# Values of three attention branches computed with the sequence on partitions, in a layer kernel on one core

## Chip, cores, metric

The kernel runs on one core of a Trainium2 chip. A core has TensorE (PE: matrix products of a stationary operand, loaded by PEld, and a moving one, into banks of PSUM), VectorE (DVE), ScalarE (ACT), GpSimd (POOL) and SyncE (SP), whose queue here issues nearly all DMAs. Each engine carries out its own instructions in order and waits at semaphores for the others. The metric is device time in microseconds.

## What is computed

One layer of a hybrid encoder, sequence S = 1024, width D = 1024, all in float32:

```python
h = rmsnorm(x, g[0])
proj = h @ w_in[l]
(mq, mk, mv, mo, mi, mf, dq, dk, dv, rq, rk, rv, rg, gates) = split_in(proj)
qk = jax.nn.silu(causal_dwconv(concatenate([mq, mk]), mlstm_conv[l]))
hm = sigmoid(mo) * head_rms(mlstm(mq_c, mk_c, mv, mi + bias, mf + bias))   # 4 heads x 256
hd = rmsnorm(diff_attention(dq, dk, dv, lam)) * (1 - lam_init)             # 8 heads, values 128
hr = silu(rg) * head_rms(retention(rq, rk, rv))                            # 4 heads x 256
y = (gm * (hm @ w_mlstm_out) + gd * (hd @ w_diff_out) + gr * (hr @ w_ret_out)) @ w_out
x = x + rmsnorm(y, g[1])
a, u = split(rmsnorm(x, g[2]) @ w_ffn_in[l])
x = x + rmsnorm((silu(a) * u) @ w_ffn_out[l], g[3])
```

mlstm and retention are scans over chunks; diff_attention is softmax attention in blocks of 128 queries.

## The kernel before

**Products.** Each float32 operand is split into a high part and the rest (`split_sbuf`, lines 104 to 106: a cast on ACT, a subtraction on DVE, tiles wh and wl), and each product is three matmuls (`mm3`, lines 108 to 113). Large products go by the seven-product scheme of Strassen and Winograd. h transposed lies on chip, hT, as seven combinations (A11, A12, S1 to S4, A22) in both parts. A `Unit` makes 256 columns of proj (heads' q, k, o or v, the gates): each of seven products takes 12 matmuls of 128x512 with weight blocks stationary and hT moving, so results have channels on partitions. Weights come in tiles ws (line 317 subtracts one from another for the scheme). Evacuations add halves, and for the mLSTM's q and k run the convolution (lines 476 and 478) on DVE.

**Order of the stages.** x is normalised and turned (lines 262 to 281), and `begin` runs the first three units, v, o and q of head 0, while the second half of x is still being turned. `gate_products` and `gate_rows` (scans on DVE for the mLSTM's gates) follow, three dense steps to each of gate_rows' steps. Then `weave(core, rate)` takes steps of twelve matmuls from `dense` (all further units, later the merges) between the steps of a core: `mlstm_core`, `ret_core` (32 chunks of 128 positions each, 2.6 dense steps to each unit of weight, two units of weight to a chunk), `diff_core`. The products after the cores (`run_last`, the FFN, `down`) fill the rest.

**Values.** v of a unit is stored with channels on partitions, beside q, k and o, in m_dram or r_dram; `chunk_of` (line 643) loads one chunk of all four, ch, one chunk ahead. `natural_v` (line 663) turns v's two 128x128 blocks on PE through `natural` (line 653), and splits the result. For the differential branch `diff_values` (lines 510 to 521) turns four blocks in each of 16 evacuations.

**What sets the order.** The Tile framework's scheduler orders every engine's instructions from the data they need and the pools they rotate through: 32 big slots, 4 for ws, 5 for weight parts, 14 half tiles s2k, and PSUM as 4 banks for the cores and 4 ("d", `psum(True)`) for dense work. `issue_after` holds work behind an instruction. In `diff_core`, `turn` (line 860) transposes the softmax weights in two groups of up to four, copied by line 870. `down` (line 1190) makes operand parts in `make` (line 1239) and runs the last operands' matmuls in line with the norm at the end.

## Time and profile before

| | us |
|---|---|
| median of 3 runs | 2622.48 (2620.74 to 2623.88) |
| the profiled execution | 2623.93 |
| its span in the trace | 2622.1 |
| TensorE busy in it | 2518.1 (96%) |
| VectorE busy | 1648.1 (63%) |
| ScalarE busy | 1250.1 (48%) |
| GpSimd busy | 335.1 (13%) |

The span is what the trace covers; the 1.8 us beside it lie outside. A busy PE is not at its peak: matmuls overlap, and their ends are modelled. So a group's mean length is no price; the distance between starts is. Stretches of the span have different limits, and each is read by itself.

### The profile page before, as it was taken

To read this page: it belongs to the slowest core of one execution; us is meant where nothing else is said; L and a number is where in the kernel's file an instruction comes from. 1 tells how busy PE (TensorE), PEld (TensorE's weight loads), DVE (VectorE), ACT (ScalarE), POOL (GpSimd) and SP (SyncE) were. 2 spreads that over 40 slices of the span, in tenths; PEclk is the share of its full clock that TensorE was granted. 3 is DMA by queue.
4 is the path that set the end of the run, shared out by engine and by line. 5 is a ranking of instruction groups with operands and counts; after the bars stand their busy time and mean duration, and the time that the engine had idled before them with its cause. 6 is when DMAs were issued, how large, how long until landed. Compare 5 with 4: busy or idle time off the path is not lost.

```text
span 2622.1 us, 35166 instructions
## 1 busy us (share of the span) xinstructions
PE 2518.1 (96%) x12061; PEld 2056.0 (78%) x12061; DVE 1648.1 (63%) x3156; ACT 1250.1 (48%) x2564; POOL 335.1 (13%) x657
## 2 busy tenths in 40 slices
PE   6999999999999999999999988999999999999997
PEld 4777887888888888888878776778877888887885
DVE  6778778666656665656556566554368655656756
ACT  6564554544444444545455555552365333334444
POOL 0011111000000000000003223332121111111000
PEclk9999999999999999999999999999999999999999
DMA  4344444444455545444476666646443333327442
GB/s 127 91 129 125 123 137 142 129 129 143 135 143 162 153 149 155 134 132 129 129 214 157 157 182 163 176 157 202 145 137 112 102 99 102 101 97 276 125 134 92
DMA packets 402077, 368.92 MB, mean 141 GB/s; under 512 B 18957, under 2 KB 302046, under 8 KB 401898
## 3 DMA queue, kind: packets, MB, share of 16 engines
q1 hardware_dynamic: 399280, 364.19, 46.3%
q10 hardware_dynamic: 2618, 2.49, 0.3%
q8 instruction: 95, 1.56, 0.3%
q14 instruction: 84, 0.69, 0.1%
HBM read 249.92 MB, written 116.69 MB: 140 GB/s over the span
## 4 chain that ended last, share of the span: by engine, by line
PE 70%; issue 10%; DVE 5%; ACT 4%; POOL 3%; DMA 3%; SPq 0%; DVEq 0%; POOLq 0%; ACTq 0%
PE ps L112 21%; PE ps L113 21%; PE ps L111 21%; PE ps L841 1%; PE ps L878 1%; ACT sb L848 1%; POOL dfac L221 1%; PE ps L694 1%; DMA s2k<-branch 1%; PE ps L653 1%; DVE wl L106 1%; DVE sb L843 1%; POOL fv L220 1%; POOL xr L208 0%; PE ps L701 0%
## 5 line engine op out<-in xcount | busy, mean ns | idle before, releaser
L105 ACT CAST wh<-ws 128x512 fp32r<-128x512 f32 (+1 forms) x622 | 385.4, 623 | 729.0 <-PE ps L112 524.8
L106 DVE TENSOR_TENSOR wl<-ws,wh 128x512 fp32r<-128x512 f32 (+1 forms) x622 | 449.9, 726 | 271.5 <-ACT wh L105 256.2
L317 DVE TENSOR_TENSOR ws<-ws,ws 128x512 f32<-128x512 f32 x234 | 161.0, 690 | 111.1 <-DMA ws<-in_w_in_dram 63.8
L111 PE MATMUL ps<-bh,wh 128*128 128x512 f32 x384 | 155.3, 404 | 0.0
L112 PE MATMUL ps<-bl,wh 128*128 128x512 f32 x384 | 152.6, 397 | 0.2 <-DVE bl L106 0.2
L113 PE MATMUL ps<-bh,wl 128*128 128x512 f32 x384 | 152.3, 397 | 0.0
L330 ACT COPY s2k<-ps 128x512 f32<-128x512 f32 x234 | 135.4, 581 | 8.7 <-PE ps L113 8.4
L111 PE MATMUL ps<-A11h,wh 128*128 128x512 f32 x312 | 127.0, 407 | 1.6 <-ACT wh L105 1.5
L113 PE MATMUL ps<-A11h,wl 128*128 128x512 f32 x312 | 125.5, 402 | 2.7 <-DVE wl L106 2.7
L111 PE MATMUL ps<-S2h,wh 128*128 128x512 f32 x312 | 125.1, 403 | 2.7 <-ACT s2k L330 2.7
L111 PE MATMUL ps<-A12h,wh 128*128 128x512 f32 x312 | 125.0, 401 | 2.2 <-DVE s2k L458 2.2
L112 PE MATMUL ps<-wl,wh 128*128 128x512 f32 x308 | 120.6, 392 | 6.1 <-DVE wl L106 6.1
L112 PE MATMUL ps<-S1l,wh 128*128 128x512 f32 x312 | 123.6, 396 | 1.6 <-DVE S1l L106 1.6
L111 PE MATMUL ps<-S3h,wh 128*128 128x512 f32 x312 | 125.1, 401 | 0.0
L112 PE MATMUL ps<-A11l,wh 128*128 128x512 f32 x312 | 124.7, 400 | 0.1
L111 PE MATMUL ps<-A22h,wh 128*128 128x512 f32 x312 | 124.8, 400 | 0.0
L112 PE MATMUL ps<-A12l,wh 128*128 128x512 f32 x312 | 123.8, 397 | 0.9 <-DVE xv L207 0.5
L111 PE MATMUL ps<-S4h,wh 128*128 128x512 f32 x312 | 124.6, 399 | 0.0
L111 PE MATMUL ps<-S1h,wh 128*128 128x512 f32 x312 | 124.1, 401 | 0.4 <-ACT S1h L105 0.3
L112 PE MATMUL ps<-S2l,wh 128*128 128x512 f32 x312 | 124.4, 399 | 0.0
L113 PE MATMUL ps<-S2h,wl 128*128 128x512 f32 x312 | 123.7, 397 | 0.0
L112 PE MATMUL ps<-A22l,wh 128*128 128x512 f32 x312 | 123.6, 396 | 0.0
(303 smaller groups left out, 6428.8 us busy)
## 6 DMA issues: line engine op xcount, KB each, us to landing
ws<-in_w_in_dram SPq DMA_DIRECT2D x112, 512.0 KB, 4.5
ws<-in_w_ffn_in_dram SPq DMA_DIRECT2D x44, 512.0 KB, 4.0
m_dram<-s2k SPq DMA_DIRECT2D x64, 256.0 KB, 2.3
ch<-m_dram SPq DMA_DIRECT2D x32, 512.0 KB, 4.4
r_dram<-s2k SPq DMA_DIRECT2D x64, 256.0 KB, 2.3
ch<-r_dram SPq DMA_DIRECT2D x32, 512.0 KB, 4.8
qk_dram<-s2k SPq DMA_DIRECT2D x64, 256.0 KB, 2.2
dk<-qk_dram SPq DMA_DIRECT2D x64, 256.0 KB, 5.9
```

The lines of the kernel that those rows point to most:

```text
L105: nc.scalar.copy(hi, src)
L106: nc.vector.tensor_sub(lo, src, hi.bitcast(F32))
L111: nc.tensor.matmul(ps, lh, rh, start=start, stop=False, skip_group_check=more)
L112: nc.tensor.matmul(ps, lh, rl, start=False, stop=False, skip_group_check=more)
L113: nc.tensor.matmul(ps, ll, rh, start=False, stop=stop, skip_group_check=more)
L220: nc.gpsimd.tensor_scalar(t, ss, scale, extra, op0=ALU.mult, op1=ALU.add)
L221: nc.gpsimd.tensor_tensor(dst, t, expo[:, 0:1], op=ALU.pow)
L317: nc.vector.tensor_sub(*sub[r])
L330: nc.scalar.copy(t, ps)
L653: nc.tensor.transpose(ps[:, j * P:(j + 1) * P], ch[:, i + j, :], ident)
L694: nc.tensor.matmul(ps[:, :P], ch[:, 2 + j, :], ch[:, j, :], start=j == 0, stop=j == 1)
L841: nc.tensor.matmul(ps[:, :b - a], d["q", qb // 4][:, c, half_cols(qb)], d["k", n][i][:, c, :b - a], start=i == 0, stop=i == 1)
```

## The change

**Values.** `natural_columns` makes the 1024 value columns of one branch with the seven products, with column slices of hT stationary and the split weights moving (128x512), so that results have the sequence on partitions. It runs for mLSTM, differential and retention values, one after another and alone, between `gate_products` and `gate_rows`, with all eight PSUM banks, and stores to mv_dram, dv_dram and rv_dram. Twelve value units of 84 matmuls go; 3 x 336 come. `natural_v` and `diff_values` lose their transposes. A chunk is loaded by two DMAs. The first three units are now o, q and k of head 0, so two of them are convolved, and the weave's rate is 2.0.

**Loads.** The first weights are loaded in the order in which `begin` uses them, behind the second half of x; the early splits of unit 0 and unit 1 no longer stand ahead of `begin`.

**Others.** The second group of `turn` uses a "d" bank; `run_last` skips a step of `turns` at i = 0; the last four operand pairs of `down` go to big slots (oh), so all are held at the end.

```diff
-    m_dram = dram.tile([MH, P, 8, S], F32, name="m_dram")
-    r_dram = dram.tile([MH, P, 8, S], F32, name="r_dram")
+    m_dram = dram.tile([MH, P, 6, S], F32, name="m_dram")
+    r_dram = dram.tile([MH, P, 6, S], F32, name="r_dram")
+    mv_dram = dram.tile([S, D], F32, name="mv_dram")
+    rv_dram = dram.tile([S, D], F32, name="rv_dram")
...
+    def natural_columns(seven, w, dst):
+        raw = [pool.tile([P, D], F32, tag="ws", bufs=N_WS, name=nm("ws")) if k < 4 else big([P, D], name="ws") for k in range(KT)]
+        for k in range(KT):
+            nc.sync.dma_start(raw[k], w[k * P:(k + 1) * P, :])
+        def right(role, k):
+            (b11, b12), (b21, b22) = ((t[:, halfs(0)], t[:, halfs(1)]) for t in (raw[k], raw[k + 4]))
+            sub = {"T1": (b12, b12, b11), "T2": (b12, b22, b12), "T3": (b11, b12, b11), "T4": (b12, b21, b12)}
+            if role in sub:
+                nc.vector.tensor_sub(*sub[role])
+                return sub[role][0]
+            return {"B11": b11, "B21": b21, "B22": b22}[role]
+        order = [(l, r, k) for l, r in (("A11", "B11"), ("A12", "B21"), ("S1", "T1"), ("S2", "T2"), ("S3", "T3"),
+                                        ("S4", "B22"), ("A22", "T4")) for k in range(4)]
+        ready = []
+        def make(n):
+            while len(ready) < min(n, len(order)):
+                _, role, k = order[len(ready)]
+                ready.append(parts_tile([P, HALF]))
+                split_sbuf(*ready[-1], right(role, k))
+        step = [0]
+        def product(ps, more):
+            for _ in range(4):
+                n = step[0]
+                make(n + 4)
+                left, _, k = order[n]
+                for j in range(4):
+                    mm3(ps[j], cols_at(seven.slot(left, k), j * P, (j + 1) * P), ready[n], k == 0 and not more, k == 3, more)
+                ready[n] = None
+                step[0] += 1
+                yield
+        def kept(ps):
+            t = [half_tile() for _ in range(4)]
+            for j in range(4):
+                nc.scalar.copy(t[j], ps[j])
+            return t
+        def out(sh, ch, ps, part):
+            for j in range(4):
+                if part is None:
+                    t = half_tile()
+                    nc.scalar.copy(t, ps[j])
+                else:
+                    t = part[j]
+                    nc.vector.tensor_add(t, ps[j], t)
+                nc.sync.dma_start(dst[(sh * 4 + j) * P:(sh * 4 + j + 1) * P, halfs(ch)], t)
+        x = [psum(True) for _ in range(4)]
+        yield from product(x, False)
+        a = kept(x)
+        y = [psum() for _ in range(4)]
+        yield from product(y, False)
+        out(0, 0, y, a)
+        y = [psum() for _ in range(4)]
+        yield from product(y, False)
+        e = kept(y)
+        yield from product(x, True)
+        b = kept(x)
+        yield from product(x, True)
+        out(1, 1, x, e)
+        yield from product(y, True)
+        out(0, 1, y, b)
+        yield from product(x, True)
+        out(1, 0, x, None)
...
-    def diff_values(hp):
-
-        def evac(j, sh, ps, part):
-            t = total(ps, part)
-            tr = psum()
-            for i in range(4):
-                nc.tensor.transpose(tr[:, i * P:(i + 1) * P], t[:, i * P:(i + 1) * P], ident)
-            v = half_tile()
-            nc.scalar.copy(v, tr)
-            c = (hp * 2 + j) * P
-            nc.sync.dma_start(dv_dram[halfs(sh), c:c + P].rearrange("(i p) e -> p i e", p=P), v.rearrange("p (i e) -> p i e", i=4))
...
-        c = u["c"]
-        nc.sync.dma_start(t, src[u["hd"]][:, :, c * P:(c + 1) * P])
+        c, hd = u["c"], u["hd"]
+        nc.sync.dma_start(t[:, 0:6, :], src[0][hd][:, :, c * P:(c + 1) * P])
+        nc.sync.dma_start(t[:, 6:8, :].rearrange("p j e -> p (j e)"), src[1][c * P:(c + 1) * P, hd * HD:(hd + 1) * HD])
...
-        ps = natural(ch, 6)
-        split_sbuf(t[:, 0, :HD], t[:, 1, :HD], ps)
+        split_sbuf(t[:, 0, :HD], t[:, 1, :HD], ch[:, 6:8, :].rearrange("p j e -> p (j e)"))
...
-        need(first + 4)
+        need(first + 3)
...
-                ps = psum()
+                ps = psum(g == 1)
...
-                        next(turns[0], None)
+                        if i > 0:
+                            next(turns[0], None)
...
-                o = [parts_tile([P, HALF]) for _ in range(2)]
+                if k < len(order) - 4:
+                    o = [parts_tile([P, HALF]) for _ in range(2)]
+                else:
+                    hl = [big([P, 2, HALF], F32R, "oh") for _ in range(2)]
+                    o = [tuple(x[:, i, :] for x in hl) for i in range(2)]
...
-        q, k, o, v = head(m_dram, (C_MQ, C_MK, C_MO, C_MV),
+        q, k, o = head(m_dram, (C_MQ, C_MK, C_MO),
                           (lambda dst, hd: convolved(dst, 2 * hd), lambda dst, hd: convolved(dst, 8 + 2 * hd),
-                           lambda dst, hd: stored(dst, AF.Sigmoid), lambda dst, hd: stored(dst)), hd)
-        units += [v, o, q, k]
+                           lambda dst, hd: stored(dst, AF.Sigmoid)), hd)
+        units += [o, q, k]
...
-        units.append(of((C_DV + hp * HD, C_DV + hp * HD + P), diff_values(hp)))
...
     units[0].load(0)
-    units[0].load(1)
     load_x(4)
-    for u in units[1:3]:
-        u.load(0)
-        u.load(1)
+    for u, i in ((1, 0), (2, 0), (0, 1), (1, 1), (2, 1)):
+        units[u].load(i)
...
-    with tc.issue_after(marks[-1].ins):
-        with tc.issue_after(lows[-1].ins):
-            units[0].split("T1")
-            units[1].split("B11", "B21")
-    begin(units[:3], hT, hx, turned(hn[4:], 1, 72, hT, hx))
+    with tc.issue_after(lows[-1].ins):
+        begin(units[:3], hT, hx, turned(hn[4:], 1, 72, hT, hx))
     hn.clear()
     made[0] = 3
     gate_products()
+    for c, dst in ((C_MV, mv_dram), (C_DV, dv_dram), (C_RV, rv_dram)):
+        for _ in natural_columns(hT, w_in[:, c:c + D], dst):
+            pass
     rows_steps = gate_rows()
     for _ in rows_steps:
         for _ in range(3):
...
                 next(dense, None)
                 owed -= 1.0
 
-    weave(mlstm_core(), 2.6)
-    weave(ret_core(), 2.6)
+    weave(mlstm_core(), 2.0)
+    weave(ret_core(), 2.0)
```

ScalarE's queue at the start, before: casts of unit 0's first weights (wh), then the high parts of hT (A11h) out of PSUM.

```order
L214 ACTIVATE junk_161,xs_162<-x_105 128x1024
L105 CAST wh_173<-ws_107 128x512
L105 CAST wh_177<-ws_107 128x512
L272 ACTIVATE A11h_187<-ps_181,pcol 128x512
L272 ACTIVATE A11h_187<-ps_192,pcol 128x512
L272 ACTIVATE A11h_206<-ps_200,pcol 128x512
```

and after:

```order
L216 ACTIVATE junk_163,xs_164<-x_107 128x1024
L107 CAST wh_175<-ws_109 128x512
L107 CAST wh_179<-ws_109 128x512
L107 CAST wh_322<-ws_119 128x512
L107 CAST wh_326<-ws_119 128x512
L274 ACTIVATE A11h_189<-ps_183,pcol 128x512
L274 ACTIVATE A11h_189<-ps_194,pcol 128x512
```

Two casts of unit 1's weights (ws_119) now stand between those of unit 0 and the first A11h.

TensorE at the start of one chunk, before; line 694 makes the scores, the two groups of line 653 turn k and v, lines 111 to 113 are dense work (S3, S4).

```order
L113 MATMUL ps_4902<-S3h_611,wl_4919 128x512
L111 MATMUL ps_4902<-S3h_611,wh_4918 128x512
L112 MATMUL ps_4902<-S3l_612,wh_4918 128x512
L113 MATMUL ps_4902<-S3h_611,wl_4919 128x512
L694 MATMUL ps_5046<-ch_4875 128x128 x2
L653 MATMUL ps_5049<-ident,ch_4875 128x128 x2
L653 MATMUL ps_5055<-ident,ch_4875 128x128 x2
L111 MATMUL ps_5007<-S4h_675,wh_4937 128x512
L112 MATMUL ps_5007<-S4l_676,wh_4937 128x512
L113 MATMUL ps_5007<-S4h_675,wl_4938 128x512
```

and after, at a chunk among A11 and A12 products (line 755 makes the scores, 715 turns k, 113 to 115 are dense):

```order
L115 MATMUL ps_8125<-A11h_208,wl_8005 128x512
L113 MATMUL ps_8125<-A11h_208,wh_8004 128x512
L114 MATMUL ps_8125<-A11l_209,wh_8004 128x512
L115 MATMUL ps_8125<-A11h_208,wl_8005 128x512
L755 MATMUL ps_8148<-ch_8008 128x128 x2
L715 MATMUL ps_8151<-ident,ch_8008 128x128 x2
L113 MATMUL ps_8167<-A12h_227,wh_8048 128x512
L114 MATMUL ps_8167<-A12l_228,wh_8048 128x512
L115 MATMUL ps_8167<-A12h_227,wl_8049 128x512
```

One pair of transposes is left between the dense steps.

TensorE's last instructions, before; ps_22673 to ps_22675 are three of the four banks that the last products fill.

```order
L113 MATMUL ps_22673<-wh_24489,wl_24488 128x512
L112 MATMUL ps_22674<-wl_24481,wh_24478 128x512
L113 MATMUL ps_22674<-wh_24480,wl_24479 128x512
L111 MATMUL ps_22674<-wh_24489,wh_24487 128x512
L112 MATMUL ps_22674<-wl_24490,wh_24487 128x512
L113 MATMUL ps_22674<-wh_24489,wl_24488 128x512
L111 MATMUL ps_22675<-wh_24480,wh_24478 128x512
L112 MATMUL ps_22675<-wl_24481,wh_24478 128x512
L113 MATMUL ps_22675<-wh_24480,wl_24479 128x512
L111 MATMUL ps_22675<-wh_24489,wh_24487 128x512
L112 MATMUL ps_22675<-wl_24490,wh_24487 128x512
L113 MATMUL ps_22675<-wh_24489,wl_24488 128x512
```

and after, where ps_22435 and ps_22436 are two of the four:

```order
L113 MATMUL ps_22435<-oh_24243 128x512
L114 MATMUL ps_22435<-oh_24244,oh_24243 128x512
L115 MATMUL ps_22435<-oh_24243,oh_24244 128x512
L113 MATMUL ps_22436<-oh_24220 128x512
L114 MATMUL ps_22436<-oh_24221,oh_24220 128x512
L115 MATMUL ps_22436<-oh_24220,oh_24221 128x512
L113 MATMUL ps_22436<-oh_24229 128x512
```

Before, a bank has the last two operands' matmuls (six) ahead of the next bank's; after, all four operands of a bank (twelve) are done before the next begins.

## Rows read from the trace of the kernel before

**Rows 1.** The page, part 1: busy us of each engine (share of the span) and instructions.

```profile
PE 2518.1 (96%) x12061; PEld 2056.0 (78%) x12061; DVE 1648.1 (63%) x3156; ACT 1250.1 (48%) x2564; POOL 335.1 (13%) x657
```

**Rows 2.** Busy time by stretch; columns: stretch, length, engines in turn, TensorE clock, DMA share, GB/s.

```profile
116.00:153.00 37.00, 28.23 (x106) 21.54 (x107) 29.79 (x57) 21.57 (x33) 6.61 (x5) 0.87 0.25 74
200.00:459.00 259.00, 251.12 (x1232) 205.53 (x1231) 201.21 (x390) 127.06 (x257) 28.65 (x106) 1.00 0.45 133
459.00:1311.00 852.00, 851.92 (x4248) 706.54 (x4247) 515.22 (x957) 406.87 (x832) 53.77 (x163) 1.00 0.48 140
1311.00:1770.00 459.00, 418.43 (x2274) 343.36 (x2273) 269.15 (x802) 250.44 (x682) 128.58 (x272) 0.99 0.63 172
```

**Rows 3.** The same view: two dense stretches, projection units and the down product.

```profile
2100.00:2300.00 200.00, 200.00 (x859) 161.15 (x858) 116.31 (x162) 70.43 (x122) 27.78 (x20) 1.00 0.32 102
2425.00:2556.00 131.00, 131.00 (x580) 108.51 (x579) 86.93 (x137) 59.67 (x106) 0.00 (x0) 1.00 0.42 130
```

**Rows 4.** Timeline of TensorE at chunk starts; columns: start us, length us, operation.

```profile
462.77 0.60 PE L694 MATMUL ps<-ch 128*128 128x128 f32 x4
...
602.00 0.61 PE L694 MATMUL ps<-ch 128*128 128x128 f32 x4
602.45 0.60 PE L653 MATMUL ps<-ident,ch 128*128 128x128 f32 x4
602.80 0.47 PE L111 MATMUL ps<-S4h,wh 128*128 128x512 f32 x1
...
802.72 0.61 PE L694 MATMUL ps<-ch 128*128 128x128 f32 x4
```

**Rows 5.** Timeline of ScalarE, VectorE and TensorE at the start; in brackets idle time before.

```profile
12.84 1.14 ACT L105 CAST wh<-ws 128x512 fp32r<-128x512 f32 x2 [1.34 <-DMA ws<-in_w_in_dram]
...
23.43 0.69 DVE L317 TENSOR_TENSOR ws<-ws,ws 128x512 f32<-128x512 f32 x1 [7.39 <-DMA ws<-in_w_in_dram]
24.04 0.74 DVE L279 TENSOR_SCALAR hx<-ps,pcol 128x512 f32<-128x512 f32 x1
...
24.84 1.12 PE L262 MATMUL ps<-ident,x 128*128 128x128 f32 x4 [7.89 <-DVE hx L279]
```

**Rows 6.** What TensorE waited for from 116 to 153 us; us, times, longest.

```profile
PE ps L113 <- DVE wl L106: 2.7, 1, 2.7
PE ps L111 <- ACT s2k L330: 2.6, 1, 2.6
PE ps L111 <- DVE s2k L458: 2.2, 1, 2.2
PE ps L111 <- ACT wh L105: 1.5, 1, 1.5
```

**Rows 7.** VectorE by line and shape, 200 to 459 us; busy us, mean ns, idle before.

```profile
L106 DVE TENSOR_TENSOR wl<-ws,wh 128x512 fp32r<-128x512 f32 x75 | 51.0, 685 | 14.3 <-ACT wh L105 13.4 <-PE ps L694 0.6
L478 DVE SCALAR_TENSOR_TENSOR s2k<-s2k,pcol,s2k 128x512 f32<-128x512 f32 x69 | 49.0, 745 | 0.2
L317 DVE TENSOR_TENSOR ws<-ws,ws 128x512 f32<-128x512 f32 x31 | 21.3, 689 | 5.0 <-DMA ws<-in_w_in_dram 4.5
...
L476 DVE TENSOR_SCALAR s2k<-s2k,pcol 128x512 f32<-128x512 f32 x23 | 10.6, 482 | 0.5 <-ACT s2k L485 0.5
...
L317 DVE TENSOR_TENSOR ws<-ws 128x512 f32<-128x512 f32 x10 | 6.9, 689 | 0.2
```

**Rows 8.** What TensorE waited for from 1311 to 1770 us, the differential stage.

```profile
PE ps L841 <- ACT s2k L870: 9.4, 14, 1.3
...
PE ps L868 <- DVE mx L843: 8.0, 4, 3.1
...
PE ps L868 <- DVE nmx L847: 1.0, 1, 1.0
```

**Rows 9.** Timeline of the tail, all engines.

```profile
2610.28 0.39 PE L113 MATMUL ps<-wh,wl 128*128 128x512 f32 x1
2610.45 2.74 DVE L1287 SCALAR_TENSOR_TENSOR x<-f,xr,x 128x512 f32<-128x512 f32 x4 [0.47 <-POOL xr L208]
...
2618.02 0.35 ACTq L1288 DMA_DIRECT2D out_dram<-x  x1
```

**Rows 10.** The chunk load's line 647, 200 to 459 us: its issues, waiters and landing.

```profile
L647 SPq DMA_DIRECT2D ch<-m_dram x16: 523/524/530, 205.9 to 450.6; - x16
...
  PE ps L694: 1.5, 2
...
DMA to landing us min/median/max: 4.3/4.4/5.0
```

**Rows 11.** TensorE by line and shape: the two kinds of transposes of values, whole span.

```profile
L653 PE MATMUL ps<-ident,ch 128*128 128x128 f32 x240 | 37.1, 273 | 2.9 <-ACT hk L772 2.9
...
L516 PE MATMUL ps<-ident,s2k 128*128 128x128 f32 x64 | 10.4, 284 | 0.0
```

**Rows 12.** Busy time by stretch, from 24 to 59 us: VectorE in the start.

```profile
24.00:59.00 35.00, 31.70 (x141) 24.12 (x141) 33.02 (x52) 27.45 (x45) 2.90 (x6) 1.00 0.10 29
```

More of the change, by code (lines that the diff above doesn't have):

```diff
@@ L507, in evac @@
                 nc.sync.dma_start(qk_dram[hd, 1 - j, i][:, halfs(sh)], t.bitcast(F32))
-        return evac
-    def diff_values(hp):
-        def evac(j, sh, ps, part):
-            t = total(ps, part)
-            tr = psum()
-            for i in range(4):
-                nc.tensor.transpose(tr[:, i * P:(i + 1) * P], t[:, i * P:(i + 1) * P], ident)
-            v = half_tile()
-            nc.scalar.copy(v, tr)
-            c = (hp * 2 + j) * P
-            nc.sync.dma_start(dv_dram[halfs(sh), c:c + P].rearrange("(i p) e -> p i e", p=P), v.rearrange("p (i e) -> p i e", i=4))
         return evac
@@ L777, in end @@
                 ml[u["hd"]].clear()
-        yield from pipelined(m_dram, 0, start, middle, end)
+        yield from pipelined((m_dram, mv_dram), 0, start, middle, end)
     def pipelined(src, first, start, middle, end):
@@ L789, in pipelined @@
             if n + 1 < len(units):
-                need(first + 4 * units[n + 1]["hd"] + 4)
+                need(first + 3 * units[n + 1]["hd"] + 3)
                 chunk_of(src, units[n + 1])
@@ L980, in end @@
                 rt[u["hd"]].clear()
-        yield from pipelined(r_dram, 4 * MH, start, middle, end)
+        yield from pipelined((r_dram, rv_dram), 3 * MH, start, middle, end)
     bT = [Act("b") for _ in range(3)]
@@ L1363, in trunk @@
     for hd in range(MH):
-        q, k, o, v = head(m_dram, (C_MQ, C_MK, C_MO, C_MV),
+        q, k, o = head(m_dram, (C_MQ, C_MK, C_MO),
                           (lambda dst, hd: convolved(dst, 2 * hd), lambda dst, hd: convolved(dst, 8 + 2 * hd),
-                           lambda dst, hd: stored(dst, AF.Sigmoid), lambda dst, hd: stored(dst)), hd)
-        units += [v, o, q, k]
+                           lambda dst, hd: stored(dst, AF.Sigmoid)), hd)
+        units += [o, q, k]
     for hd in range(MH):
-        units += head(r_dram, (C_RQ, C_RK, C_RG, C_RV),
-                      (lambda dst, hd: stored(dst), lambda dst, hd: stored(dst),
-                       lambda dst, hd: stored(dst, AF.Silu), lambda dst, hd: stored(dst)), hd)
+        units += head(r_dram, (C_RQ, C_RK, C_RG),
+                      (lambda dst, hd: stored(dst), lambda dst, hd: stored(dst), lambda dst, hd: stored(dst, AF.Silu)), hd)
     for hp in range(DH // 2):
```

## The prediction

> **What bounds the kernel now.** The page first: TensorE is busy for 2518.1 us, 96% of the span [rows 1], so the reader should look for matmul time that goes and for the few stretches in which TensorE waits. The stretches come next [rows 2]. From 459 to 1311 us, where the mLSTM and retention chunks are woven with the projections, TensorE is busy for 851.92 of 852.00 us at a granted clock of 1.00 (the 2.4 GHz level): nothing but fewer or denser instructions helps there. Idle time lies in four places: the start, 116 to 153 us (8.8 us idle, clock 0.87), 200 to 459 us (7.9 us idle, VectorE busy for 201.21 of 259 us) and the differential stage from 1311 us on (40.6 us idle). The sum below is made against the profiled execution, 2623.9 us with 2622.1 of span; it lies 1.4 us above the median of the runs, 2622.5 us, to which the result is compared. About 0.2%, 5 us, is what a measurement of this kernel can tell from no change.
>
> **The transposes that go, −17 us.** Values are made with the sequence on partitions, so the 64 chunks of mLSTM and retention lose two 128x128 transposes each, and the differential values lose 64: 192. They lie in TensorE's full stretches, so nothing hides them. Those of the chunks are shown as 273 ns long [rows 11], but that is a latency: instructions overlap. What counts is from start to start: the four transposes at 602.45 are followed by a matmul at 602.80, so four take 0.35 us, 0.0875 each [rows 4]. 192 x 0.0875 = 16.8 us. The gain is no smaller, since all lie among matmuls without a gap; were each worth its whole duration, that would be a rival, below. The 128 evacuating passes that read those banks are not saved: the split of v stays, and reads the loaded chunk itself.
>
> A rule speaks for that rival. The Trainium skill, "TensorE: Matmul & The Clock Gate", section "Part 4: PE-mode transpose", gives about 275 ns for a 128x128 transpose inside a kernel. The durations agree (273 ns), the spacing does not; by the rule as a price the term would be 192 x 0.275 = 52.8 us instead of 16.8.
>
> **The matmuls of the values, −6 us.** Twelve value units of 84 matmuls (1008) leave the woven stream, and 3 x 336 = 1008 of the same size run by themselves after the start. The count is unchanged; the spacing is not quite. Projection units issue 859 matmuls in 200.00 us, 0.2328 each; the down product, whose stationary operands are slices of activations and whose moving operands are weight parts as here, issues 580 in 131.00 us, 0.2259 each [rows 3]. Taking 0.2266, near the second since the form is its, gives 1008 x 0.0062 = 6 us. The low end is −7, at the down product's spacing. The high end is +4: at the entry of each of the three passes the first split may not be ready, and such a wait of PE for a cast cost 1.5 us at the present place [rows 6]; 3 x 1.5 − 0.5. Weight loads should not bind: all sixteen slots are loaded by SP ahead of the pass. Each pass needs 28 splits (a cast on ScalarE and a subtraction on VectorE at 685 ns [rows 7]) for 28 x 12 x 0.2266 = 76 us, so VectorE is half free even with the evacuations.
>
> **The start, −3 us.** Before, VectorE's queue holds a subtraction on weights (line 317) which waits 7.39 us for its load and ends at 24; behind it stands hx, and PE waits 7.89 us for hx at 24.84 [rows 5]. The change no longer forces that subtraction early, and loads first what the first unit needs. But in the new order ScalarE has two casts of unit 1's weights ahead of the A11 evacuations. Their load is the tenth in its queue; the eighth-or-later load that releases line 317 now lands at 23.4, the first ones are cast at 12.84 [rows 5], so 10.6 us pass for some seven loads, and a load two to three places sooner lands at about 20 (an estimate from these two rows). The stall moves from VectorE to ScalarE and shortens by 3 us. Ends: 7.9 (it vanishes) and 0 (it is only renamed).
>
> **116 to 153 us, −7 us.** There gate_rows' scans and the convolved pieces stand on VectorE together with the first units' splits. 106 matmuls at 0.233 need 24.7 of 37 us; 12.3 are lost: 8.8 of idle time (the longest wait 2.7 for wl; 1.5 for wh [rows 6]) and 3.5 at the lower clock [rows 2]. After, the convolution of two units still falls together at the end of begin, but 228 us of value products with slack on VectorE lie between it and the scans, and the scans meet the chunk loop's first units only. I take 5 of the 12.3 as left. Ends: −12 (all gone) and +2 (two convolved units at begin's end in place of one, 4 more pieces of three line-478 and one line-476 operations, 2.7 us each on VectorE [rows 7], partly covered).
>
> **VectorE beside the chunks, +6 us.** This is the term against the change. In 200 to 459 us there are 259 / 17.0 = 15.2 chunks (20 chunk starts lie between 462.77 and 802.72 [rows 4]). VectorE's 13.2 us per chunk are: splits and weight subtractions (51.0 + 21.3 + 6.9) / 15.2 = 5.2; convolution (49.0 + 10.6) / 15.2 = 3.9; the rest, core and additions, 4.1 [rows 2, 7]. A chunk takes two turns of weave, so 5.2 steps of twelve matmuls before and 4 after. The period falls to 17.0 − 1.2 x 12 x 0.233 − 0.18 = 13.5 us. Splits shrink to 4.0; convolution does not, because two units in three (not in four) are convolved: 3.9 x 0.77 x 4/3 = 4.0. Sum 12.1 of 13.5 us, 90% against 78%. In stretches of q and k alone it is 4.0 + 6.0 + 4.1 = 14.1 of 13.5, 105%; before 5.2 + 7.8 + 4.1 = 17.1 of 17.0. Nine units of the mLSTM remain for the loop, six of them convolved: 6 x 7 / 4 = 10.5 chunk periods x 0.6 = 6 us. Ends: 0 (buffers carry the excess into the o units) and +14 (the present 7.9 us of idle time doubles on top). At the retention units nothing is convolved and VectorE has room.
>
> **The differential turn, −3 us.** The second group of transposes takes a bank of the dense half. PE waits 9.4 us for ScalarE's copies out of line 870 before line 841, and 8.0 for VectorE's mx [rows 8]; the bank removes part of the first kind alone, and the maximum is then the next to be late. Ends: −9.4, and +4 if the woven merges wait for the borrowed bank (two waits of the mean length of those for mx, 2.0 [rows 8]).
>
> **The tail, −1.5 us.** The last matmul starts at 2610.28, the last store is issued at 2618.02 [rows 9]; the span ends 4.1 us after. With the last operands in large slots, the four banks finish 12 matmuls apart (2.7 us by the down product's spacing), not six, so the first halves' passes move under TensorE; two rows' chain behind the last bank stays. The 2.74 us of four pieces [rows 9] suggest that half of it moves. Ends: −3 and 0.
>
> **At nothing.** Two DMAs per chunk instead of one: a chunk is loaded one ahead, 13.5 us, and lands 4.4 us after issue [rows 10]; what it costs if that cover goes is a rival. run_last's skipped step: the scheduler leaves the transposes in the same place. The stores of v go to tensors of their own: same bytes, on the same queue.
>
> **Sum.** −17 − 6 − 3 − 7 + 6 − 3 − 1.5 = −31.5, so 2623.9 − 31.5 = 2592.4 in the profiled run, **2591 us** against the median.
>
> **VectorE covered.** VectorE keeps up with the chunks, and the stalls at the start and at 116 us vanish: 6 + 4.9 + 5.3 more, 2575 us. For it: the o units and deep pools; against: in-order queues that now stand at 78%.
> **VectorE the bound.** It sets the pace beside q and k. Its best stretch reaches 33.02 of 35.00 us, 94% [rows 12]; 14.1 / 0.94 = 15.0 us per chunk, 1.5 over the period, x 10.5 = +16 instead of +6, and then the scans at 116 us only move: 7 more. 2608 us.
> **Late chunks, slower than before.** The chunk loads come late. SP issues in order, behind stores that wait for evacuations; it must issue each chunk's two loads within 13.5 − 4.4 = 9 us. From there on every chunk waits. The two waits now seen are 0.75 us each on average (1.5 in two [rows 10]); on 64 chunks that is +48: 2639 us. Against: these are the only two in 259 us.
> **Whole durations.** Each removed transpose frees its whole duration: 192 x 0.273 = 52.4 in place of 16.8: 2555 us. Against it stands the spacing in [rows 4]. The rule of the Trainium skill cited above would come out here.
>
> **Chances.** Forecast 0.60, its own range 2575 to 2608 (bounds added as squares). VectorE covered 0.16. VectorE the bound 0.13. Late chunks 0.07. Whole durations 0.04. The range for 8 in 10 leaves out the last two and the outer ends: 2567 to 2613. Faster (under 2617.2): 0.60 + 0.16 + 0.04 and 0.07 of the 0.13, less 0.01: 0.86. Within 0.2%: 0.06, the outer part of the VectorE case and of the forecast. Slower: 0.08.
>
> **What would show it.** Chunk starts 13.5 us apart, and two instead of four transposes of 128x128 behind the score pair; 1008 matmuls in about 228 us without idle time; the first long wait of PE on ScalarE, ending near 21 us; the loss before the chunk loop at 5 us or less; VectorE at about 90% beside the mLSTM chunks, with waits of PE for wl and s2k of some 14 us; the last matmul within 10 us of the end. Wrong would be shown by waits for ch, by idle time between passes, or by a spacing above 0.23 in the value stage.

## Result, and the profile after

The changed kernel takes 2596.4 us (median of four, 2595.2 to 2599.1) against 2623.2 (2620.7 to 2624.0): 0.9895 of the time before, 95% interval 0.9882 to 0.9908, 26.8 us less. The forecast was 2591, in a range of 2567 to 2613. The profiled executions have spans of 2622.1 and 2594.0 us, 28.1 apart.

The page's part 1, kernel after (answers to [rows 1]):

```profile
PE 2492.9 (96%) x11869; PEld 2037.9 (79%) x11869; DVE 1637.6 (63%) x3156; ACT 1245.4 (48%) x2550; POOL 335.2 (13%) x657
```

TensorE has 192 instructions fewer, and 25.2 us of the 28.1 are its busy time. The share of 96% is unchanged: the kernel is bound as before, by a shorter list.

Busy time by stretch, after: value products, the rest up to the first chunk, the first sixteen chunks (here and below, from the first one's start to the sixteenth's), the other chunks, the differential stage (columns as in [rows 2]).

```profile
98.00:336.00 238.00, 238.00 (x1045) 195.03 (x1045) 124.68 (x211) 83.99 (x142) 0.10 (x1) 1.00 0.31 98
336.00:393.00 57.00, 55.70 (x247) 44.45 (x246) 43.01 (x70) 36.23 (x56) 1.51 (x8) 1.00 0.48 142
393.00:622.00 229.00, 213.63 (x1051) 175.31 (x1050) 178.95 (x361) 119.57 (x251) 30.91 (x108) 0.98 0.42 128
622.00:1290.00 668.00, 666.25 (x3365) 556.33 (x3364) 431.57 (x834) 346.06 (x722) 54.45 (x161) 1.00 0.51 153
1327.00:1715.00 388.00, 350.36 (x1975) 289.63 (x1975) 239.88 (x752) 218.96 (x618) 120.32 (x260) 0.99 0.64 169
```

The same view of the kernel before, in its own stretches from gate_products to the first chunk, sixteen chunks, the other chunks, the differential stage:

```profile
105.00:176.00 71.00, 62.06 (x259) 48.40 (x259) 45.27 (x87) 38.61 (x64) 6.71 (x6) 0.93 0.38 112
176.00:447.00 271.00, 263.12 (x1293) 215.54 (x1292) 212.40 (x413) 135.31 (x274) 30.71 (x113) 1.00 0.42 125
447.00:1295.00 848.00, 847.92 (x4225) 703.14 (x4225) 512.01 (x954) 404.30 (x826) 52.89 (x161) 1.00 0.48 142
1351.00:1740.00 389.00, 350.77 (x1976) 289.23 (x1974) 239.63 (x751) 219.53 (x617) 119.72 (x260) 0.99 0.63 169
```

The value products have no idle time at all. The loss before the first chunk is gone (8.9 us of idle time to 1.3, clock 0.93 to 1.00), and a loss of about the same size has come up among the first sixteen chunks: 15.4 of 229 us, where 7.9 of 271 stood before.

What TensorE waited for in the chunks beside the convolved units, 393 to 646 us after (us, times, longest):

```profile
PE ps L113 <- issue: 8.1, 3, 3.6
PE ps L755 <- DMA ch<-m_dram: 2.1, 2, 1.2
PE ps L762 <- ACT hk L833: 1.8, 2, 1.1
PE ps L113 <- ACT s2k L332: 1.7, 2, 1.2
```

The line "issue" names no releaser, so the timelines of the engines have to be read beside each other. TensorE, VectorE and ScalarE at one such wait, after:

```profile
573.91 0.36 PE L113 MATMUL ps<-s2k,s2k 128*128 128x258 f32 x1 [2.42 <-issue]
...
569.95 0.74 DVE L552 SCALAR_TENSOR_TENSOR s2k<-s2k,pcol,s2k 128x512 f32<-128x512 f32 x1
...
571.01 0.74 DVE L552 SCALAR_TENSOR_TENSOR s2k<-s2k,pcol,s2k 128x512 f32<-128x512 f32 x1
...
572.00 0.74 DVE L552 SCALAR_TENSOR_TENSOR s2k<-s2k,pcol,s2k 128x512 f32<-128x512 f32 x1
572.66 0.42 DVE L800 SCALAR_TENSOR_TENSOR s2k<-ch,wib 128x256 f32<-128x256 f32 x1
...
573.32 0.49 ACT L107 CAST s2k<-s2k 128x384 fp32r<-128x384 f32 x1
```

The waiting matmul is the first of a chunk's products; it needs the weights w of the scores, 384 wide, split in two parts. Line 800 makes the last of w only at 572.66, behind three operations of the convolution (line 552, 478 before), ScalarE's cast of w ends at 573.8, and TensorE starts at 573.91. So VectorE's queue is late here, though VectorE is busy for only 78% of the stretch (178.95 of 229 us).

Of the two other nameless waits, the one of 2.00 us that ends at 467.04 shows the same pattern. The longest, 3.65 us up to 417.30, does not:

```profile
413.69 1.28 ACT L534 ACT_TABLE_LOAD   x1
...
415.12 0.41 DVE L800 SCALAR_TENSOR_TENSOR s2k<-ch,wib 128x256 f32<-128x256 f32 x1
...
416.69 0.51 ACT L107 CAST s2k<-s2k 128x384 fp32r<-128x384 f32 x1
...
417.30 0.55 PE L113 MATMUL ps<-s2k,s2k 128*128 128x258 f32 x1 [3.65 <-issue]
```

There line 800 is done at 415.53, with no convolution right ahead of it, and the cast of w comes only at 416.69: in ScalarE's queue it stands behind a table load of 1.28 us and four other operations. So the late queue is ScalarE's in this wait, and the convolution is at most an indirect cause.

The start, after: ScalarE, then TensorE (answers to [rows 5]).

```profile
13.64 1.14 ACT L107 CAST wh<-ws 128x512 fp32r<-128x512 f32 x2 [1.65 <-DMA ws<-in_w_in_dram]
20.61 1.14 ACT L107 CAST wh<-ws 128x512 fp32r<-128x512 f32 x2 [5.83 <-DMA ws<-in_w_in_dram]
21.66 1.83 ACT L274 ACTIVATE A11h<-ps,pcol 128x512 fp32r<-128x512 f32 x3
...
22.39 1.22 PE L113 MATMUL ps<-A11h,wh 128*128 128x512 f32 x2 [5.27 <-ACT A11h L274]
```

The stall has changed its engine: casts of unit 1's weights wait 5.83 us for their load, and A11h stands behind them.

The tail, after (answers to [rows 9]): 8.7 us from the last matmul's start to the end of the span, against 11.9.

```profile
2585.31 0.39 PE L115 MATMUL ps<-oh,oh 128*128 128x512 f32 x1
...
2589.03 1.42 DVE L1353 SCALAR_TENSOR_TENSOR x<-f,xr,x 128x512 f32<-128x512 f32 x2 [0.73 <-POOL xr L210]
2590.47 0.35 ACTq L1354 DMA_DIRECT2D out_dram<-x  x1
```

### The profile page after: what moved, and what is told of

Same layout as the page of the kernel before. It is cut to its first block, busy times and chain, and to the rows that moved or that the text cites. A ratio compares the mean times of both kernels' runs of the same rounds, so it can differ in the third digit from the quotient of the medians.

```text
span 2594.0 us, 34769 instructions
## 1 busy us (share of the span) xinstructions
PE 2492.9 (96%) x11869; PEld 2037.9 (79%) x11869; DVE 1637.6 (63%) x3156; ACT 1245.4 (48%) x2550; POOL 335.2 (13%) x657
## 4 chain that ended last, share of the span: by engine, by line
PE 55%; issue 8%; DVE 3%; ACT 3%; POOL 3%; DMA 2%; SPq 0%; POOLq 0%; DVEq 0%; ACTq 0%
PE ps L114 17%; PE ps L115 17%; PE ps L113 17%; PE ps L939 2%; PE ps L902 1%; DMA s2k<-branch 1%; POOL dfac L223 1%; PE ps L755 1%; PE ps L929 1%; ACT sb L909 1%; ACT s2k L909 0%; DVE sb L904 0%; POOL xr L210 0%; POOL fv L222 0%; ACT wh L107 0%
## 5 line engine op out<-in xcount | busy, mean ns | idle before, releaser
L319 DVE TENSOR_TENSOR ws<-ws,ws 128x512 f32<-128x512 f32 x198 | 135.8, 689 | 101.0 <-DMA ws<-in_w_in_dram 54.6
L332 ACT COPY s2k<-ps 128x512 f32<-128x512 f32 x198 | 114.9, 581 | 14.1 <-PE ps L115 13.9
L115 PE MATMUL ps<-wh,wl 128*128 128x512 f32 x292 | 113.7, 389 | 0.0
L113 PE MATMUL ps<-A11h,wh 128*128 128x512 f32 x264 | 106.9, 406 | 5.3 <-ACT A11h L274 5.3
L113 PE MATMUL ps<-wh,wh 128*128 128x512 f32 x292 | 111.2, 389 | 0.0
L113 PE MATMUL ps<-S2h,wh 128*128 128x512 f32 x264 | 105.8, 401 | 1.2 <-ACT s2k L332 1.2
L115 PE MATMUL ps<-S3h,wl 128*128 128x512 f32 x264 | 105.6, 400 | 0.0
L114 PE MATMUL ps<-S3l,wh 128*128 128x512 f32 x264 | 105.4, 399 | 0.0
L114 PE MATMUL ps<-A12l,wh 128*128 128x512 f32 x264 | 104.7, 396 | 0.8 <-DVE xv L209 0.6
L115 PE MATMUL ps<-A11h,wl 128*128 128x512 f32 x264 | 105.1, 398 | 0.1
```

The source lines that it names most:

```text
L113: nc.tensor.matmul(ps, lh, rh, start=start, stop=False, skip_group_check=more)
L114: nc.tensor.matmul(ps, lh, rl, start=False, stop=False, skip_group_check=more)
L115: nc.tensor.matmul(ps, ll, rh, start=False, stop=stop, skip_group_check=more)
L319: nc.vector.tensor_sub(*sub[r])
L332: nc.scalar.copy(t, ps)
```

## The experiments

Times below are medians; the kernel before was measured beside each group, at 2624.2 to 2624.4 us in three of them and 2623.8 in the other. Single runs of one kernel mostly lie within 3 us of their median, a few up to 5.8, so single medians do not settle differences below about 3 us. "Idle" is the sum of TensorE's idle times in a stretch of the profiled execution.

**One part undone: the bank in the differential turn.**

```diff
-                ps = psum(g == 1)
+                ps = psum()
```

> The changed kernel (2596.4 us, 0.9895 of the time before) with one part undone: the second group of transposes in the differential turn takes a bank of the cores again. Theory: the bank gave nothing, because the idle time of the differential stage stood at 37.4 us before and 37.5 after; the time stays within 1.5 us of 2596.4. Rival: the bank gained the forecast 3 us and the woven merges gave them back, so that undoing it alone costs about 3 us (2599).

2597.5 us (2593.8 to 2599.2), ratio 0.9896 (0.9882 to 0.9909): not told apart from the changed kernel. Its differential stage, from the first to the last score product, takes 392.2 us against 388.5. Over all kernels of this study the stage takes 389.3 to 392.2 with the old bank (four kernels, mean 390.2) and 385.7 to 389.9 with the new one (ten, mean 387.9). By these means the bank is worth about 2 us; no single comparison of times shows it.

**One part undone: down's large slots.**

```diff
-                if k < len(order) - 4:
+                if k < len(order):
```

> The changed kernel with one part undone: the last four operand pairs of down go to the rotating parts again. Theory: the tail grows from 8.7 us between the last matmul's start and the end back to 11.8, 3.1 us more, 2599.5 in all. Rival: the tail shortens because of something else, and the time stays at 2596.4.

2597.4 us, ratio 0.9898 (0.9885 to 0.9912). The tail grows to 11.3 us from 8.7 as expected, and VectorE's last pass is again four pieces in a row:

```profile
2588.87 2.74 DVE L1353 SCALAR_TENSOR_TENSOR x<-f,xr,x 128x512 f32<-128x512 f32 x4 [0.47 <-POOL xr L210]
```

The median rises by 1.0 only, less than it can tell. All kernels with the slots end 8.2 to 8.8 us after the last matmul's start, all without 11.1 to 11.9.

**The stall at the start, taken away.**

```diff
+    with tc.issue_after(marks[-1].ins):
+        with tc.issue_after(lows[-1].ins):
+            units[1].split("B11", "B21")
     with tc.issue_after(lows[-1].ins):
         begin(units[:3], hT, hx, turned(hn[4:], 1, 72, hT, hx))
```

> The changed kernel with one wait taken away at the start: the split of unit 1's first weights is held behind the marks of hT's first half, so that ScalarE's first casts after unit 0's are A11's, and no 5.3 us wait for the tenth load stands ahead of them. Theory 1: the stall was the whole loss of the start; TensorE's first dense matmul comes at about 17 and the time falls by 4 to 5 us to 2592. Theory 2: the start is bound by the loads of weights and of x, the stall moves to a later product of begin, and the time changes by less than 1.5 us.

2587.6 us, ratio 0.9859 (0.9846 to 0.9873): 8.8 us less, more than the wait itself. ScalarE now goes on to A11h without a load in between, and TensorE's first dense matmul starts at 16.12 in place of 22.39:

```profile
13.91 1.14 ACT L107 CAST wh<-ws 128x512 fp32r<-128x512 f32 x2 [2.19 <-DMA ws<-in_w_in_dram]
15.38 1.84 ACT L274 ACTIVATE A11h<-ps,pcol 128x512 fp32r<-128x512 f32 x3 [0.33 <-PE ps L264]
...
16.12 0.80 PE L113 MATMUL ps<-A11h,wh 128*128 128x512 f32 x1
```

Up to the first value product the idle time falls from 21.9 to 14.0 us. Later waits of `begin` (S1l 1.8 us, for one, now 0.6) shrank with it. Theory 1 holds, and its price was too small.

**More dense work beside the convolved units.**

```diff
-            owed += rate * w
+            owed += (2.6 if made[0] < 3 * MH else rate) * w
...
-    weave(mlstm_core(), 2.0)
-    weave(ret_core(), 2.0)
+    weave(mlstm_core(), 1.9)
+    weave(ret_core(), 1.9)
```

> The changed kernel with another rate of weaving: 2.6 dense steps per unit of weight, as before the change, as long as units of the mLSTM are left (the convolved ones among them), and 1.9 after. The work is the same. Theory (cover): the 17 us of idle time beside the convolved units come from fewer dense matmuls between a chunk's scores and its products, while the convolution stands ahead of the chunk's own steps on VectorE; with 2.6 the idle time goes back to about 8 and the time falls by 9 to 11 us to about 2586. Rival 1 (VectorE's load): VectorE is the bound beside q and k, at 105% in the prediction's count against 101% with 2.6, so only 2 to 3 us come back. Rival 2: the idle time moves to the later chunks, where the rate is now 1.9, and nothing is gained.

2584.1 us, ratio 0.9844 (0.9831 to 0.9857): 12.3 less, as the theory of the cover has it. The idle time of the first sixteen chunks is 7.9 us instead of 15.4, and what is left of the nameless waits is 3.2 (397 to 650 us, one chunk more):

```profile
397.00:650.00 253.00, 245.13 (x1202) 201.32 (x1201) 195.50 (x390) 137.01 (x277) 29.68 (x116) 0.99 0.44 132
...
PE ps L113 <- issue: 3.2, 2, 2.4
```

VectorE's share is 77%, against 78% in the stretch of the kernel after: its load is the same, and TensorE waits half as long. The two stretches differ in one thing: with 2.6 the convolved units are done after 9 chunks and not after 12. So the same view from the first chunk to the end of the last convolved piece, kernel after and then this one:

```profile
393.00:572.70 179.70, 166.34 (x805) 135.56 (x803) 145.47 (x290) 96.00 (x199) 24.41 (x84) 0.97 0.40 121
396.90:559.10 162.20, 156.44 (x748) 127.16 (x747) 133.61 (x259) 94.24 (x186) 17.40 (x69) 0.99 0.39 120
```

VectorE's share rises from 81% to 82%, and TensorE's idle time falls from 13.4 to 5.8 us, from 1.1 to 0.6 us a chunk. So VectorE's load was not the cause of this part. More dense matmuls now lie between a chunk's scores and its products, and fewer chunks stand beside the convolution; the idle time a chunk speaks for the first, but no run separates the two. The later chunks, with 1.9, did not wait more (1.5 against 1.7 us).

**Transposes put back, 112 of them, read by nobody.**

```diff
-        ps = natural(ch, 2)
+        ps = psum()
+        for j in range(2):
+            nc.tensor.transpose(ps[:, j * P:(j + 1) * P], ch[:, 2 + j, :], ident)
+        for j in range(2, 4):
+            nc.tensor.transpose(ps[:, j * P:(j + 1) * P], ch[:, 4 + j, :], ident)
+        ps = ps[:, :HD]
```

> The changed kernel with 112 transposes put back whose result nobody reads: behind each chunk's two transposes of k (112 of them in the trace, in 56 chunks) the chunk's two blocks of v are transposed as well, into the other half of the same bank. Nothing else is added, no evacuation and no load. By the spacing of the rows, 0.0875 us each, the time rises by 9.8 us over the changed kernel's 2596.4; by the intervals of all removed groups in the two traces, 21 us for 192, 0.109 each, by 12.2; by their whole length of 273 ns, the rival with the Trainium skill's rule (TensorE: Matmul & The Clock Gate, Part 4: PE-mode transpose), by 30.6.

2605.2 us, ratio 0.9928 (0.9914 to 0.9941): 8.9 more, 0.079 each, with some 3 us of uncertainty. That excludes 30.6 and does not tell 9.8 from 12.2. The timeline does better. The added pair starts at 649.18, and the next matmul at 649.31; without it (kernel after, at 634.66) the matmul comes 0.14 us behind k's pair:

```profile
648.96 0.38 PE L721 MATMUL ps<-ident,ch 128*128 128x128 f32 x2
649.18 0.38 PE L723 MATMUL ps<-ident,ch 128*128 128x128 f32 x2
649.31 0.48 PE L113 MATMUL ps<-S1h,wh 128*128 128x512 f32 x1
```

0.35 − 0.14 = 0.21 us for two, 0.105 each, while each row shows 273 ns an instruction as before. From pair to pair it is 0.22 us, 0.11 each; a pair before a dense matmul shows 0.13 to 0.14, with v's pair or without. The 0.0875 of the prediction is a group's length, with this short last step in it, divided by four. The rule of the Trainium skill ("TensorE: Matmul & The Clock Gate", "Part 4: PE-mode transpose", about 275 ns in a kernel) agrees with the length in the rows and is no price for the time: the measured 0.08 to 0.11 us decides.

**Two of the convolution's taps left out, kernel after.**

```diff
-            for i in (2, 1, 0):
+            for i in (2,):
```

> The changed kernel with two of the three shifted taps of the convolution left out (the output is not the reference's): each convolved piece takes 1.2 us of VectorE in place of 2.7; PE, loads and the rates are the same. Theory: the idle time in the first sixteen mLSTM chunks (15.3 us and 2.7 at the lower clock) comes from chunk steps that stand behind the convolution in VectorE's queue; it falls to 9 or less and the time by 8 to 11 us to about 2587. Rival: the waits come from the chunk's own chain (ScalarE's casts, GpSimd's factor), whatever stands on VectorE; the time changes by less than 3 us.

2572.4 us, ratio 0.9802 (0.9788 to 0.9815): 24.0 less, twice and more what was expected. The first sixteen chunks keep 2.9 us of idle time:

```profile
385.00:597.00 212.00, 209.08 (x1055) 174.72 (x1055) 155.04 (x322) 121.81 (x247) 28.24 (x105) 1.00 0.45 137
```

The direction is the theory's. The size is not, since `begin` (4.0 us shorter) and the stretch before the chunks (4.1 shorter) gained as well.

**The same two taps left out of the kernel before.** The edit is the same line.

> The kernel before with two of the three shifted taps of the convolution left out (the output is not the reference's), as b2_one_tap does in the changed kernel, where that gave 24 us. Theory: the convolution on VectorE cost the kernel before as well, both in the stretch from 104 us to the first chunk (12.4 us of idle time and lower clock, beside gate_rows' scans) and in the first chunks (7.7): the first falls to 4 or less and the second to 2 or less, 13 to 16 us in all, so the change made the convolution dearer by some 8 to 11 us. Rival: the stall before the chunks is the scans' own, it stays at 9 or more, and only 5 to 8 us go.

2604.0 us, ratio 0.9924 (0.9905 to 0.9943): 20.3 less. The stall before the first chunk goes nearly whole, and so do the waits in the first chunks:

```profile
102.00:164.00 62.00, 60.24 (x271) 48.30 (x270) 40.79 (x80) 36.53 (x63) 1.40 (x6) 1.00 0.42 129
164.00:427.00 263.00, 260.75 (x1294) 216.36 (x1293) 184.27 (x366) 135.98 (x274) 29.80 (x113) 1.00 0.43 129
```

In both stretches the idle time is about 2 us (8.9 and 7.9 with the whole convolution). The scans alone stall next to nothing, so the rival falls. The gain was again larger than expected. With 24.0 after and 20.3 before, the change made the convolution dearer by some 4 us and not by 8 to 11; with the uncertainty of both medians, 4 us are not clear of nothing.

**The values alone, and the three other parts alone.** The first is the changed kernel with load order, early splits, turn's bank and down's slots as before; the second is the kernel before with those of the change.

> The values alone: the changed kernel with the order of loads and early splits, the bank in the differential turn and the slots of down as before the change. Theory: nearly all of the gain is the values' (transposes 21 us, spacing of matmuls 4, the stall before the chunk loop 11, less 12 beside the convolved units); the three other parts are worth 1 us each or nothing, so the time is 2597 to 2600. Rival: the parts hang together, and without the others the values give less than 20 of the 26.8 us (over 2603).

> The kernel before with the three other parts alone: the new order of loads without the early splits, the new bank in the differential turn and the large slots of down; values made as before. Theory: about 1 us for the bank, 1 for the slots, nothing at the start, so 2620 to 2623 against 2624.4. Rival: the start gains the forecast 3 us with these units, and the turn its 3, so 2616 or less.

The values alone: 2605.5 us (2601.0 to 2606.3), ratio 0.9928 (0.9914 to 0.9941), 18.8 less than before, 15 to 23 by the interval. The small parts alone: 2615.1, ratio 0.9970 (0.9959 to 0.9982), 9.2 less, 5 to 11 by the interval. The sum, 28.0, meets the 26.8 of the whole change: the parts add, within these intervals, and do not hang together as the rival has it. But the shares are not those expected: the values give less, the small parts 9 and not 3. In the small parts' trace the stages have shrunk by 3.6 us (differential), 3.0 (tail), 1.3 (the products before it), 1.7 (before the first chunk) and 0.8 (start), and the chunks have grown by 1.5. Undone singly in the changed kernel, bank and slots cost 1 us each in the medians; how 9 us and 1 + 1 go together is not settled, beyond the scatter of medians by 2 to 3 us.

**Both improvements together, and two steps further.** The first joins the run that takes the stall at the start away (a3_start_casts) and the run with more dense work beside the convolved units (a4_rate_by_units). The second adds this:

```diff
-            nc.vector.tensor_scalar(r, t[:, 3:], tap[3], None, op0=ALU.mult)
+            nc.scalar.activation(r, t[:, 3:], AF.Copy, scale=tap[3])
```

The third has 4.0 and 1.8 for the rates 2.6 and 1.9.

> Both improvements of the changed kernel together: unit 1's split behind the marks of hT's first half, and 2.6 steps as long as mLSTM units are left, 1.9 after. Theory: they act on different stretches and add: 2596.4 - 8.8 - 12.2 = 2575. Rival: the earlier start only reaches the convolved units sooner, and half of it is lost again there: 2580.

> As c1_start_and_rate, with the first of the convolution's four operations (0.48 us on VectorE, line 476 of the kernel before) made by ScalarE as a copy with a scale. Theory: what stands ahead of the chunk's steps on VectorE shrinks from 2.7 to 2.2 us a piece, a third of what the two taps left out took away (1.5 us a piece, 24 us in all), so 5 to 8 us more: 2568 to 2570. Rival: ScalarE has the same chunks' casts behind it in its queue, the wait moves there, and the time stays within 2 us of c1_start_and_rate's or rises.

> As c1_start_and_rate with 4.0 steps as long as mLSTM units are left and 1.8 after. Theory (cover): still more dense matmuls lie between a chunk's scores and its products, so the last 7.8 us of idle time among the first sixteen chunks fall to 4 or less, 3 to 5 us less than c1_start_and_rate. Rival: with fewer chunks among the convolved units the convolution fills VectorE by itself (9.6 us of splits and additions and 10.3 of convolution per unit of 19.6 us of TensorE), and TensorE waits for weight parts; as slow as c1_start_and_rate or slower.

Both together: 2574.3 us, ratio 0.9812 (0.9798 to 0.9825), the sum of the two gains within the uncertainty, and 49.5 us below the kernel before. With the first tap on ScalarE: 2577.4, ratio 0.9824 (0.9810 to 0.9837). The idle time of the sixteen chunks falls from 7.9 to 6.3 us, but the first value product comes 5.4 us later (94.9 us for 89.5), with 18.9 us of idle time ahead of it in place of 15.5 and 10.2 us at the lower clock in place of none. TensorE's wait for ScalarE's S1h there grows from 0.8 to 3.7 us. The rival is right that relief on VectorE is paid on ScalarE, though it shows in `begin` and not in the chunks. With 4.0 steps: 2573.6, ratio 0.9812 (0.9799 to 0.9825), no different from 2.6. Beside the convolved units the idle time falls from 5.6 to 0.8 us, with VectorE busy for 84% there (82% with 2.6), as the theory of the cover has it. But in the first sixteen chunks together it is 5.5 us, and in the others it rises from 1.6 to 5.6: it moved to the later chunks, which have the lower rate. The rival has the time right and the reason wrong.

## Why the prediction was right, step by step

The time fell into the forecast's own range; the sum was −31.5 for the profiled execution and the spans differ by 28.1. That the total came so close is in part luck: single terms missed by 2 to 7 us, in both directions. (The low end of the range, by bounds added as squares, comes to 2580 and not to 2575; the result lies inside either.) By terms:

- **Transposes, −17.** Between starts of TensorE's rows the groups of lines 653 and 516 took 28.8 us before (without two waits inside them), and the group that is left (line 715) 7.8 after: −21.0. The reading by starts was right. What failed in the step was its only row: 0.35 us for four includes the short last step to the dense matmul. Starts inside a group lie 0.11 us apart, and 192 x 0.11 is 21. Whole durations (−52) were wrong.
- **The matmuls of the values, −6.** 1008 matmuls in 238.9 us less 8.2 for the gate's in between are 0.229 each, against 0.2328: about −4. The down product's 0.2259 was not reached. No entry of a pass cost a wait.
- **The start, −3.** The mechanism was right to the place: ScalarE's casts wait for the tenth load until 20.61 us (about 20 was estimated). TensorE's long wait ends at 22.39 in place of 24.84, 2.5 us sooner. The step that failed is its balance: idle time and lower clock up to the first value product (up to gate_products before) are 23.6 us against 21.8, +1.8, because `begin` loses the gain again. Its other units are the reason, as far as single profiles tell: the values alone, with the same units and the old order of loads, lose 26.2 us there, so the order gave 2.6 of its 3; and the kernel after without two taps loses 19.3, so the convolution of a second unit in `begin`, which this term left out, took the rest. The run without the stall (a3_start_casts) shows what stood there for the taking: 8.8 us.
- **Before the chunks, −7, and VectorE beside the chunks, +6.** Measured: 12.6 us of idle time and lower clock to 1.3, −11.3; and 8.0 to 20.9 in all chunks, +12.9. (The lower clock's part is worked out from 128x512 matmuls that start 0.427 us apart in place of 0.233: 3.6 us before, 3.8 after.) The two terms were costed as two causes; they are one. Without two taps both kernels lose nearly all of it, wherever it stood: the convolution's cost moved from the gates' stretch into the chunk loop, and the net of the two was +1.6 where −1 was forecast. The step that failed in the second is the reckoning by VectorE's load: 90% was forecast, 78% measured with twice the waits, and the run with 2.6 steps (a4_rate_by_units) takes away half of the waits at the same load. VectorE's work was sized well, 11.9 us a chunk for 12.1; it did not set the pace. As far as the waits read above and the rates tell, it was position in an in-order queue (VectorE's, and ScalarE's in the longest wait) and thin cover that made the loss, 4.0 steps to a chunk instead of 5.2. The period of the later chunks is 13.95 us on average where 13.5 was forecast: the 17.0 it starts from divides 19 periods by 20 starts, and the later chunks before take 17.7 us on average.
- **The differential turn, −3.** The stage went from 389.3 to 388.5 us, −0.8; by the means over all kernels the bank is worth 2.
- **The tail, −1.5.** 11.9 to 8.7, −3.2, just past the far end of its bounds: the last pass of VectorE fell from four pieces to two, and POOL's and the norm's steps of the first rows went under TensorE as well.
- **Two DMAs per chunk, nothing.** The waits for ch before line 755 are 2.1 us in all chunks (1.5 before [rows 10]), so the late chunks of the rival do not come; the larger of the two loads lands after 3.7 us.

These terms sum to −25.6; another 1.1 is idle time after the cores (15.7 to 14.6), and the rest, 1.4 us, is not assigned. The rival in which VectorE is the bound had the right place and the wrong measure: nothing of it needs VectorE's share to be near 100%.

## What to carry to other kernels

Work that is taken from an interleaved stream also takes away cover: the chunk loop lost 1.2 steps a chunk, and the waits came where the chain of a chunk was longest, at an engine that was idle for a fifth of the time. A rate of interleaving should follow what runs beside it, not be one number. And a load wait that is removed from one in-order queue should be looked for in the others: the scheduler had put it on ScalarE, where moving two casts behind a few short operations was worth 9 us.

## What the runs showed of the hardware

Float32 transposes of 128x128 in a row started 0.11 us apart (a pair behind a pair in 0.22 us, 648.96 to 649.18), while their rows show 273 ns each; 112 of them added cost 8.9 us. The last start of a group lies closer to the next dense matmul's, so a short group's length divided by its number is too low a price.

Within the idle time of 3.65 us that ended at 417.30 us the granted clock fell to 0.50, the lower level of 1.2 GHz, and it came back to 1.00 while TensorE was busy. The window at the lower level, and three matmuls in it, 0.42 to 0.43 us apart:

```profile
415.50:422.30 6.80, 5.00 (x16) 4.41 (x17) 4.40 (x10) 3.71 (x9) 0.00 (x0) 0.50 0.88 247
...
419.37 0.63 PE L113 MATMUL ps<-S3h,wh 128*128 128x512 f32 x1
419.79 0.63 PE L114 MATMUL ps<-S3l,wh 128*128 128x512 f32 x1
420.22 0.63 PE L115 MATMUL ps<-S3h,wl 128*128 128x512 f32 x1
```

It fell once more from 524.7 to 528.1 us, behind an idle time of 1.21 us. In the first sixteen chunks the lower clock cost about 3.8 us beside 15.4 of idle time (the expectation for the kernel after without two taps has 2.7 and 15.3).
